# Delta rule: where a tile's convolution and the values' eviction stand in the order of the engines

## The chip, the cores and the metric

The kernel runs on one core of a Trainium2 chip. The core has TensorE (PE, matrix products), VectorE (DVE), ScalarE (ACT), GpSimd (POOL) and SyncE (SP, which issues DMA transfers); each executes its own queue in order, and semaphores tie the queues together. The metric is the device time of one execution, in microseconds (us): 3261.68 as the median of 3 runs (3260.92 to 3266.36).

## The reference, cut to what matters

One inference step of a two-layer recurrent trunk, over a prompt of 2048 tokens and 8 sample tokens. The first layer (gated linear attention beside a state-space model) is not touched. The second layer is a gated delta rule with 8 heads of width 128:

```
qkv, z, b, a = split((h @ w_in).astype(f32), ODD_SIZES)
qkv, conv_new = causal_conv(qkv, s_conv, conv_w)     # depthwise, width 4
qkv = silu(qkv)
q, k, v = split(qkv);  q = l2norm(q) * DN_DK ** -0.5;  k = l2norm(k)
beta = sigmoid(b);  g = -exp(a_log) * softplus(a + dt_bias)
# per chunk of tokens:
lower = where(strict, beta * (k k^T) * decay, 0)
sol = triangular_solve(lower + eye, [v * beta, k * beta * exp(gcum)])
v_new = u_v - w_k S
o = (q * exp(gcum)) S + (q k^T * decay) v_new
S = S * exp(g_last) + (k * exp(g_last - gcum))^T v_new
out = (rmsnorm(o) * silu(z)) @ w_out
```

## The kernel before, in words

The prompt is cut into four blocks of four chunks of 128 tokens. The first block also carries the 8 sample tokens, so its dense products run in two sub-tiles of 264 and 256 columns; the others have one sub-tile of 512. A step is one head of one block: 32 steps, heads 0 to 7 of each block. Weights and activations are split in a high and a low half, so a dense product of 8 blocks of the inner dimension is 24 matrix multiplications per sub-tile (`dense_steps`; `Hh`, `Hl` are the activations, `whl` the weights).

`dn_dense` makes, for one step, four products in the order k, q, v, z. For k, q and v, `project` allocates the tile `pre`, copies the three columns before the block into it (`pre<-halo`, L1675; in the first block also `pre<-cst`, L1673), lets ACT evict the product from PSUM into it (L1682), and then makes the convolution: one scaled copy on ACT (L1690), three multiply-adds on DVE (L1692, tile `yc`), a tanh on ACT (L1695, tile `th`, which shares its two buffers with `pre`), and the product that gives `kT`, `qT` or `vT` (L1696). So a next `pre` can be filled only when the convolution before has read the buffer two allocations back. The products use two PSUM banks (`pmm`): PE can start a sub-tile only when the one two before it has been evicted.

`dn_prefix` (per step) turns kT by PE transposes, builds `MT`, sends a diagonal `md` through DRAM and back (`LB`), and runs a chain of 30 small DVE instructions (`t`, `u`). `dn_inverse` makes the triangular inverse, `dn_queries` turns qT and vT by PE transposes into `ptp` banks (two of them) and evicts the values as `vtok` (L1838), `dn_chain` runs the chunk recurrence (`pch`, `ppo`, `xx`, `dS`), and `dn_sample` treats the sample tokens (its states are updated by eight DVE instructions, `sbuf`, L2037).

The order on PE is fixed by a planner (`Weave`): each piece of work is a generator that yields what it waits for, and the planner runs the next one that is due on a clock that counts PE work alone, at 2400 columns per us; `weave.post(key, after)` makes a piece due `after` us of that clock later, with numbers from the table `LAT`. In `dense_steps` each of the 8 steps of a sub-tile yields once. The order on the other engines comes from the scheduler of the framework, which places an instruction by priority and its own timing; `in_turn()` takes that freedom from an instruction: it may not be placed ahead of the DVE instruction that was given out last before it. `after(steps, late)` runs a product and, once four yields have passed with something in the list `late`, gives out the first entry of that list.

Of the kernel before, what the change touches and what calls it, by code (L numbers as in the profile page):

```python
# [12 lines left out]
F32 = mybir.dt.float32  # L13
# [4 lines left out]
AF = mybir.ActivationFunctionType  # L18
OP = mybir.AluOpType
# [4 lines left out]
P = 128  # L24
D = 1024
KD = 8
EPS = 1e-6
NSM = 8
# [7 lines left out]
C3 = float(np.float32(TWO_PI - C1 - C2))  # L36
MAGIC = 12582912.0

LAT = dict(gates=11, conv=5, kconv=8, snorm=5.25, z=2.04, tp=3, qtp=1, mt=18, grow=5, blocks=9, sub=3, dve=1.02, act=0.675,
           gchain=0.9, gload=1.2, gsample=15, columns=0.9, hout=3, gsplit=3.57, inv1=1.53, inv2=1.3, inv3=0.9,  # L40
           inv4=0.837, inv5=0.796, inv6=0.972, chain1=0.972, chain2=0.729, chain3=0.837, split=1.95, sload=2.66,
           cout=2.25, norm=5.5, load=2, us=3.74, sq=4, out=3.24, entry=9.6, x=1.88, gentry=7.98, make=30, far=8,
# [97 lines left out]
def tile_trunk(ctx, tc, A, O):  # L140
    nc = tc.nc
# [6 lines left out]
    TG = NSM + P * GBLK[0][1]  # L148
# [99 lines left out]
    convw = cvec[:, 19:115].rearrange("p (i t) -> p t i", t=24)  # L248
# [384 lines left out]
    weave = Weave(tc, pe)  # L633
# [916 lines left out]
    w_odd = A["w_in_odd"][0]  # L1550
    dS, keep = [], {}
# [106 lines left out]
    def dn_dense(dp, blk, h, g):  # L1658
        hi, lo = H[blk]
        ns, off, T, subs = bounds(blk)  # L1660
        nch = blk[1]
        X0 = NX if ns else 3
        kT = dp.tile([P, NCG, P], F32, tag="kT", bufs=3, name="kT")
        qT = dp.tile([P, NCG, P], F32, tag="qT", bufs=3, name="qT")
        kqs = dp.tile([P, 3, NSM], F32, tag="kqs", bufs=2, name="kqs") if ns else None
        zs = dp.tile([P, TG], F32, tag="zs", bufs=3, name="zs")
        dd[g] = [kT, qT, kqs, None, zs]

        def project(ti, dst, si):
            pre = dp.tile([P, NX + TG - NSM], F32, tag="pre", bufs=2, name="pre")  # L1670
            W = X0 + nch * P
            if ns:
                nc.vector.tensor_copy(pre[:, :32].rearrange("p (s i) -> p s i", i=4)[:, :, :3],  # L1673
                                      keep["cst"][:, ti].rearrange("p i s -> p s i"))
            nc.vector.tensor_copy(pre[:, X0 - 3:X0], halo[:, :, ti])  # L1675

            def ev(ps, o, w, c, k):
                n0 = ns if c == 0 else 0
                if n0:
# [8 lines left out]
            y = dp.tile([P, NX + TG - NSM], F32, tag="yc", bufs=2, name="yc")  # L1688
            yv = y[:, 3:W]
            nc.scalar.activation(yv, pre[:, 0:W - 3], AF.Copy, scale=convw[:, ti, 0:1])  # L1690
            for i in range(1, 4):
                nc.vector.scalar_tensor_tensor(yv, pre[:, i:W - 3 + i], convw[:, ti, i:i + 1], yv,  # L1692
                                               op0=OP.mult, op1=OP.add)
            t = dp.tile([P, NX + TG - NSM], F32, tag="pre", bufs=2, name="th")
            nc.scalar.activation(t[:, 3:W], yv, AF.Tanh, scale=0.5)  # L1695
            nc.vector.scalar_tensor_tensor(dst, t[:, X0:W].rearrange("p (c t) -> p c t", t=P), 1.0,  # L1696
                                           y[:, X0:W].rearrange("p (c t) -> p c t", t=P),
                                           op0=OP.add, op1=OP.mult)
            if ns:
                s4 = lambda a: a[:, :32].rearrange("p (s i) -> p s i", i=4)[:, :, 3]  # L1700
                nc.vector.scalar_tensor_tensor(kqs[:, si], s4(t), 1.0, s4(y), op0=OP.add, op1=OP.mult)

        yield from project(8 + h, kT[:, :nch], 0)
        weave.post(("k", g), LAT["kconv"])
        yield from project(h, qT[:, :nch], 1)
        weave.post(("q", g), LAT["conv"])
# [3 lines left out]
        yield from project(16 + h, vT[:, :nch], 2)  # L1710
        weave.post(("v", g), LAT["conv"])
# [6 lines left out]
        yield from dense_steps(w_odd[:, 3072 + h * P:3072 + (h + 1) * P], KD, hi, lo, subs, ev_z)  # L1718
        weave.post(("z", g), LAT["z"])

    def tiles_of(n):
# [99 lines left out]
    def dn_queries(dp, blk, h, g):  # L1821

        n = blk[1]
        kT, qT, kqs, vT, zs = dd[g]
        eg, E, ktok, ivr, cb, egl = keys[g]
        T3 = tiles_of(n)
        pt = ptp()
        for c in range(n):
            pe.transpose(pt[:, c * P:(c + 1) * P], qT[:, c], ident)
        rq = norms(pt, n, "sq_")[1]  # L1830
        rq_ = dp.tile([P, NCG], F32, tag="rq", bufs=3, name="rq")[:, :n]
        nc.vector.tensor_scalar(rq_, rq, P ** -0.5, None, op0=OP.mult)
# [5 lines left out]
        nc.vector.tensor_tensor(vtok, pt[:, :n * P].rearrange("p (c t) -> p c t", t=P),  # L1838
                                ivr.unsqueeze(2).to_broadcast([P, n, P]), op=OP.mult)
# [501 lines left out]
```

## Time and profile before

| what | us |
|---|---|
| median of 3 runs | 3261.68 |
| lowest and highest | 3260.92, 3266.36 |
| the profiled execution's own time | 3250.56 |
| its span in the trace | 3248.8 |
| the delta-rule layer's head steps | about 1738 to 3172 |
| of these the first block | about 1738 to 2110 |

The profile is one execution. Its page gives busy times of each engine, its trace every instruction. PE is busy for 91% of the span, DVE for 68%. A wait is shown as the idle time of an engine ahead of an instruction, with the instruction on another engine that ended it. PEclk is the clock that was granted to TensorE: 1.00 is 2.4 GHz, 0.50 is 1.2 GHz.

### The profile page before, as it was taken

The page shows a single profiled execution, that of the slowest core. Times are in us where ns is not written, and L with a number is a line of the kernel's source. Part 1 is how long each engine was busy: PE and PEld are TensorE (multiplying, and loading weights), DVE is VectorE, ACT ScalarE, POOL GpSimd, SP SyncE. Part 2 cuts the span into 40 slices and gives each one's busy share as a digit, 9 for nine tenths or more (in the row PEclk, how much of TensorE's full clock was granted, in tenths as well). Part 3 has the DMA queues.
Part 4 walks back from the last instruction along what each step waited for, and adds up shares of the span by engine and source line. Part 5 has one row for each costly group of instructions (what it writes and reads, how often), then busy time and mean ns, then how long its engine had stood idle before and what let it go on. Part 6 is the DMA issues. An engine that isn't in the chain of part 4 may idle for free.

```text
span 3248.8 us, 53026 instructions
## 1 busy us (share of the span) xinstructions
PE 2955.9 (91%) x18425; PEld 2497.5 (77%) x18425; DVE 2224.4 (68%) x5715; ACT 1255.7 (39%) x3321; POOL 995.0 (31%) x1236
## 2 busy tenths in 40 slices
PE   6888799999999989978988888899998999999998
PEld 5877678777778768877767888877887788787886
DVE  7766556645444546765867888867887678857885
ACT  5443343323323323241134444443444344434442
POOL 6565444322202222240034444431112121211111
PEclk8898899999999999989999999999999999999999
DMA  7565965673483485664466566676444844475446
GB/s 216 190 209 177 297 184 148 190 256 126 136 276 126 133 287 153 200 202 148 155 198 216 172 193 185 190 230 221 139 147 140 270 146 145 125 234 192 141 139 191
DMA packets 398232, 602.96 MB, mean 186 GB/s; under 512 B 62521, under 2 KB 257964, under 8 KB 397828
## 3 DMA queue, kind: packets, MB, share of 16 engines
q1 hardware_dynamic: 394902, 589.98, 57.3%
q0 software_dynamic: 2560, 8.42, 0.9%
q8 instruction: 145, 2.38, 0.3%
q10 hardware_dynamic: 502, 1.17, 0.1%
q14 instruction: 123, 1.01, 0.1%
HBM read 433.31 MB, written 166.34 MB: 185 GB/s over the span
## 4 chain that ended last, share of the span: by engine, by line
PE 35%; DVE 15%; DMA 4%; issue 3%; ACT 2%; POOL 1%; SPq 0%; POOLq 0%; DVEq 0%; ACTq 0%
PE pmm L93 23%; PE prc L93 5%; PE ptp L97 2%; PE pch L93 2%; DVE yc L1692 2%; PE ppo L93 2%; DVE z L1237 1%; DVE z L1247 1%; DVE Hl L649 1%; DMA out<-yt 1%; DMA LB<-md_d 1%; DVE z L1243 1%; DMA whl<-split 1%; DVE z L1238 0%; DVE z L1248 0%
## 5 line engine op out<-in xcount | busy, mean ns | idle before, releaser
L93 PE MATMUL pmm<-Hh,whl 128*128 128x512 f32 (+4 forms) x5200 | 1597.3, 370 | 42.8 <-ACT pre L1682 13.2
L93 PEld LDWEIGHTS pmm<-Hh,whl 128*128 128x128 f32 x5200 | 951.2, 193 | 173.8 <-ACT pre L1682 14.8
L93 PE MATMUL pmm<-Hl,whl 128*128 128x512 f32 (+5 forms) x2640 | 937.0, 355 | 5.6 <-DVE Hl L649 4.2
L93 PEld LDWEIGHTS pmm<-Hl,whl 128*128 128x128 f32 (+1 forms) x2640 | 506.5, 192 | 55.6 <-DVE Hl L649 6.0
L93 PE MATMUL pmm<-Oh,whl 128*128 128x512 f32 (+2 forms) x1120 | 354.3, 379 | 30.5 <-DVE res L1064 13.4
L320 POOL TENSOR_TENSOR whl<-raw,whl 128x512 fp32r<-128x512 f32 (+1 forms) x176 | 232.3, 1322 | 203.9 <-ACT whl L319 194.9
L93 PEld LDWEIGHTS pmm<-Oh,whl 128*128 128x128 f32 x1120 | 211.3, 200 | 65.7 <-DVE res L1064 16.9
L1692 DVE SCALAR_TENSOR_TENSOR yc<-pre,cvec,yc 128x512 f32<-128x512 f32 (+1 forms) x288 | 228.8, 795 | 43.2 <-ACT yc L1690 40.5
L93 PE MATMUL pmm<-Ol,whl 128*128 128x512 f32 (+2 forms) x560 | 203.3, 363 | 0.6 <-DVE Ol L370 0.6
L319 ACT ACTIVATE whl<-raw 128x512 fp32r<-128x512 f32 (+1 forms) x176 | 108.5, 618 | 127.4 <-PE pmm L93 78.0
L93 PEld LDWEIGHTS pmm<-Ol,whl 128*128 128x128 f32 x560 | 112.6, 201 | 11.4 <-DVE Ol L370 1.7
L907 DVE TENSOR_TENSOR dlt<-b 128x512 f32<-128x512 f32 x112 | 87.5, 782 | 39.8 <-ACT E L914 38.9
L93 PE MATMUL pmm<-oh,whl 128*128 128x512 f32 (+3 forms) x320 | 93.6, 370 | 18.3 <-DVE res L1378 15.4
L908 ACT ACTIVATE E<-dlt 128x256 f32<-128x256 f32 x112 | 47.4, 423 | 156.1 <-DVE dlt L907 32.3
L1682 ACT ACTIVATE pre<-pmm 128x512 f32<-128x512 f32 (+1 forms) x120 | 61.1, 510 | 115.4 <-PE pmm L93 115.1
L646 POOL TENSOR_TENSOR xb<-xb,rr 128x1024 f32<-128x1024 f32 (+1 forms) x32 | 76.9, 2412 | 90.9 <-DMA xb<-xs_d 40.4
L1968 ACT ACTIVATE jk<-ppo,rq 128x128 bf16<-128x128 f32 x128 | 46.7, 365 | 140.2 <-PE ppo L93 139.1
L1685 POOL COPY halo<-pre 128x3 f32<-128x3 f32 x96 | 22.3, 232 | 241.0 <-ACT pre L1682 240.3
L1064 DVE TENSOR_TENSOR res<-pmm,res 128x512 f32<-128x512 f32 (+2 forms) x80 | 46.2, 584 | 68.6 <-PE pmm L93 50.0
L1729 ACT ACTIVATE jk<-ptp 128x128 bf16<-128x128 f32 x256 | 70.8, 277 | 53.8 <-PE ptp L97 48.3
L275 POOL TENSOR_TENSOR s<-s,mhalf 128x4 f32<-128x4 f32 (+2 forms) x41 | 40.6, 989 | 162.6 <-DVE s L274 160.7
L1695 ACT ACTIVATE th<-yc 128x512 f32<-128x512 f32 (+1 forms) x96 | 61.0, 635 | 73.1 <-DVE yc L1692 72.8
(1527 smaller groups left out, 6103.8 us busy)
## 6 DMA issues: line engine op xcount, KB each, us to landing
whl<-split SPq DMA_DIRECT2D x460, 512.0 KB
split<-whl SPq DMA_DIRECT2D x168, 512.0 KB
res<-xs_d SPq DMA_DIRECT2D x88, 256.0 KB
sm<-s5m SPq DMA_DIRECT2D x32, 514.0 KB
raw<-in_w_in_even SPq DMA_DIRECT2D x64, 256.0 KB
xs_d<-res SPq DMA_DIRECT2D x64, 256.0 KB
raw<-in_w_in_odd SPq DMA_DIRECT2D x64, 256.0 KB
LB<-md_d SPq DMA_DIRECT2D x64, 256.0 KB
```

The costliest lines, as they stand in the source:

```text
L93: return self.e.matmul(out, w, x, **kw)
L97: return self.e.transpose(out, x, ident)
L319: nc.scalar.activation(t[:, 0, :m], raw, AF.Copy)
L320: nc.gpsimd.tensor_tensor(t[:, 1, :m], raw, t[:, 0, :m].bitcast(F32), op=OP.subtract)
L646: nc.gpsimd.tensor_tensor(xb, xb, rr.unsqueeze(1).to_broadcast(list(xb.shape)), op=OP.mult)
L907: nc.vector.tensor_tensor(d3, b3, b3[:, :, s - 1:s].to_broadcast([P, nb_, 2 * s]), op=OP.subtract)
L908: nc.scalar.activation(E3[:, :, s:], d3[:, :, s:], AF.Exp, scale=IS)
L1682: nc.scalar.activation(pre[:, X0 + c * P:X0 + (c + k) * P], ps[:, n0:], AF.Copy)
L1692: nc.vector.scalar_tensor_tensor(yv, pre[:, i:W - 3 + i], convw[:, ti, i:i + 1], yv, op0=OP.mult, op1=OP.add)
L1695: nc.scalar.activation(t[:, 3:W], yv, AF.Tanh, scale=0.5)
L1729: nc.scalar.activation(jk, pt[:, c * P:(c + 1) * P], AF.Square, accum_out=ss[:, c:c + 1])
L1968: nc.scalar.activation(jk[:rows], po[:rows, c * P:(c + 1) * P], AF.Square, scale=rq[:rows, c:c + 1], accum_out=s1[:, c:c + 1])
```

## The change

Three edits, all in the delta-rule layer.

```diff
-LAT = dict(gates=11, conv=5, kconv=8, ...
+LAT = dict(gates=11, conv=4, kconv=6.5, ...
...
-        def project(ti, dst, si):
-            pre = dp.tile([P, NX + TG - NSM], F32, tag="pre", bufs=2, name="pre")
+        late = []
+
+        def project(ti, dst, si, done):
             W = X0 + nch * P
-            if ns:
-                nc.vector.tensor_copy(pre[:, :32]..., keep["cst"]...)
-            nc.vector.tensor_copy(pre[:, X0 - 3:X0], halo[:, :, ti])
+            pre_ = []
             def ev(ps, o, w, c, k):
+                if c == 0:
+                    pre_.append(dp.tile([P, NX + TG - NSM], F32, tag="pre", bufs=2, name="pre"))
+                pre = pre_[0]
+                if c == 0:
+                    if ns:
+                        nc.vector.tensor_copy(pre[:, :32]..., keep["cst"]...)
+                    nc.vector.tensor_copy(pre[:, X0 - 3:X0], halo[:, :, ti])
...
-            yield from dense_steps(w_odd[:, ti * P:(ti + 1) * P], KD, hi, lo, subs, ev)
+            yield from after(dense_steps(w_odd[:, ti * P:(ti + 1) * P], KD, hi, lo, subs, ev), late)
...
+            def turn():
                 nc.scalar.activation(yv, pre[:, 0:W - 3], AF.Copy, scale=convw[:, ti, 0:1])
-            for i in range(1, 4):
+                with in_turn():
+                    nc.vector.scalar_tensor_tensor(yv, pre[:, 1:W - 2], convw[:, ti, 1:2], yv, ...)
+                for i in range(2, 4):
                     nc.vector.scalar_tensor_tensor(yv, pre[:, i:W - 3 + i], convw[:, ti, i:i + 1], yv, ...)
...
+                weave.post((done, g), LAT["kconv" if done == "k" else "conv"])
+            late.append(turn)
...
-        yield from dense_steps(w_odd[:, 3072 + h * P:...], KD, hi, lo, subs, ev_z)
+        yield from after(dense_steps(w_odd[:, 3072 + h * P:...], KD, hi, lo, subs, ev_z), late)
...
             pe.transpose(pt[:, c * P:(c + 1) * P], vT[:, c], ident)
-        nc.vector.tensor_tensor(vtok, pt[...], ivr..., op=OP.mult)
+        yield LAT["qtp"]
+        with in_turn():
+            nc.vector.tensor_tensor(vtok, pt[...], ivr..., op=OP.mult)
```

The convolution of a product is given out at the fourth yield of the product behind it (k's amid q, q's amid v, v's amid z); its first DVE instruction may not stand ahead of DVE work given out until then. `pre` is allocated, and its halo copied, at the first eviction. The planner's due time for kT is now 6.5 us of its clock after that fourth yield (before: 8 after the product's end), for qT and vT 4 (before: 5). The eviction `vtok` is given out one due time (`qtp`, 1 us) after vT's transposes, and marked in the same way; the product of q and k that follows it moves with it. Every engine executes the same instructions as before; only their order differs. In the changed kernel L1692 is L1702 and L1705, L1675 is L1684, L1838 is L1853, L2037 is L2052.

The order on PE, head 0 of the first block, from the last matrix multiplication of v's product (256 columns) to vT's transposes, before:

```order
L93 MATMUL pmm<-Hh,whl 128x256
L93 MATMUL pmm<-Hh,whl 128x264
L93 MATMUL pmm<-Hl,whl 128x264
L93 MATMUL pmm<-Hh,whl 128x264
L97 MATMUL ptp<-ident,vT 128x128 x4
L93 MATMUL prc<-qT,kT 128x128 x4
```

and now, with z's first sub-tile (264 columns) from its third multiplication on:

```order
L93 MATMUL pmm<-Hh,whl 128x264
L97 MATMUL ptp<-ident,qT 128x128 x4
L93 MATMUL pmm<-Hh,whl 128x264
L93 MATMUL pmm<-Hl,whl 128x264
L93 MATMUL pmm<-Hh,whl 128x264 x2
L93 MATMUL pmm<-Hl,whl 128x264
L93 MATMUL pmm<-Hh,whl 128x264 x2
L93 MATMUL pmm<-Hl,whl 128x264
L93 MATMUL pmm<-Hh,whl 128x264 x2
L93 MATMUL pmm<-Hl,whl 128x264
L93 MATMUL pmm<-Hh,whl 128x264
L97 MATMUL ptp<-ident,vT 128x128 x4
```

Before, vT's transposes stood 3 multiplications behind the end of v's product; now they stand 15 behind it.

The order on DVE, head 1 of the first block, from q's convolution to the halo copy that lets v's product be evicted, before (`sbuf` are the sample states of head 0):

```order
L1692 SCALAR_TENSOR_TENSOR yc<-pre,cvec,yc 128x544
L2037 SCALAR_TENSOR_TENSOR sbuf__17516<-sbuf__17516,egs,sbuf__17517 128x128 x8
L1692 SCALAR_TENSOR_TENSOR yc<-pre,cvec,yc 128x544
L1731 TENSOR_SCALAR sk__17820<-sk__17820 128x4
L1776 TENSOR_TENSOR ktok<-ptp,E 128x512
L1692 SCALAR_TENSOR_TENSOR yc<-pre,cvec,yc 128x544
L1673 COPY pre<-cst 128x8x3
L1675 COPY pre<-halo 128x3
```

and now, the rows from these sample states to q's convolution:

```order
L2052 SCALAR_TENSOR_TENSOR sbuf__17510<-sbuf__17510,egs,sbuf__17511 128x128 x8
L1709 SCALAR_TENSOR_TENSOR kT<-th,yc 128x512
L1828 TENSOR_TENSOR t__17557<-LB,u__17555 128x4x5
L370 TENSOR_TENSOR Ol<-og,Oh 128x8
L1714 SCALAR_TENSOR_TENSOR kqs<-th,yc 128x8
L1768 COPY egs<-gr 128x8
L1771 COPY egl<-gr 128x4
L1702 SCALAR_TENSOR_TENSOR yc<-pre,cvec,yc 128x544
L1830 TENSOR_TENSOR u__17555<-u__17555,t__17557 128x4x5
L2029 TENSOR_TENSOR kq<-i_75,kqs 128x2x32
L1705 SCALAR_TENSOR_TENSOR yc<-pre,cvec,yc 128x544
```

The eight updates of the sample states stood between the first and the second multiply-add of q's convolution; now they stand ahead of kT, and of q's convolution.

The order on DVE, head 1 of the first block, from vT to vtok before:

```order
L1696 SCALAR_TENSOR_TENSOR vT<-th,yc 128x512
L1701 SCALAR_TENSOR_TENSOR kqs<-th,yc 128x8
L1799 TENSOR_TENSOR lb<-MT,blkd 128x512
L1716 SCALAR_TENSOR_TENSOR zs<-thr,pmm 128x264
L1801 TENSOR_REDUCE md<-lb 128x64
L1731 TENSOR_SCALAR sq__17959<-sq__17959 128x4
L1716 SCALAR_TENSOR_TENSOR zs<-thr,pmm 128x256
L1838 TENSOR_TENSOR vtok<-ptp,ivr 128x512
L1832 TENSOR_SCALAR rq<-rn 128x4
L1845 TENSOR_TENSOR kq__17999<-prc,E 128x512
```

and now, the rows that end in vtok and U:

```order
L1993 TENSOR_TENSOR on<-so,s_18169 8x128
L1830 TENSOR_TENSOR u__18061<-u__18061,t__18063 128x4x4
L1948 SCALAR_TENSOR_TENSOR xx__18221<-pch,neg,vtok 128x128
L1828 TENSOR_TENSOR t__18063<-LB,u__18061 128x4x3
L1830 TENSOR_TENSOR u__18061<-u__18061,t__18063 128x4x3
L1828 TENSOR_TENSOR t__18063<-LB,u__18061 128x4x2
L1830 TENSOR_TENSOR u__18061<-u__18061,t__18063 128x4x2
L1828 TENSOR_TENSOR t__18063<-LB,u__18061 128x4
L1830 TENSOR_TENSOR u__18061<-u__18061,t__18063 128x4
L1853 TENSOR_TENSOR vtok<-ptp,ivr 128x512
L1873 TENSOR_TENSOR U<-blkd,u__18061 128x512
```

The eviction of the values stood seven rows behind vT, ahead of the chain of `t` and `u`; now it stands behind that chain.

## Rows read from the trace of the kernel before

**Rows 1.** Busy time by stretch: columns in the heading line.
```profile
core 0: us, PE busy (x) PEld busy (x) DVE busy (x) ACT busy (x) POOL busy (x), PEclk, DMA share, GB/s
1738.00:2110.00 372.00, 323.22 (x2755) 305.05 (x2755) 320.97 (x935) 171.72 (x541) 170.83 (x183) 0.96 0.60 188
2430.00:2610.00 180.00, 165.63 (x973) 133.75 (x971) 122.88 (x309) 72.66 (x196) 32.33 (x38) 0.98 0.63 201
2610.00:2790.00 180.00, 179.50 (x1217) 150.75 (x1216) 145.99 (x424) 79.92 (x243) 34.17 (x45) 1.00 0.47 143
```

**Rows 2.** Waits of PE, 1735 to 2110: us in total, times, longest.
```profile
PE pmm L93 <- ACT pre L1682: 13.2, 5, 6.7
PE pch L93 <- DVE dS L1950: 8.5, 7, 2.4
...
PE ptp L97 <- DVE vT L1696: 2.7, 1, 2.7
```

**Rows 3.** Waits of PE, 2610 to 2790.
```profile
PE ppo L93 <- ACT jk L1968: 0.3, 1, 0.3
```

**Rows 4.** Waits of DVE, 1735 to 2110.
```profile
DVE yc L1692 <- ACT yc L1690: 9.7, 7, 6.2
DVE vtok L1838 <- PE ptp L97: 3.9, 3, 1.7
```

**Rows 5.** Timeline of DVE, start of the first block: start, us, instruction, idle before.
```profile
1734.27 1.28 DVE L1692 SCALAR_TENSOR_TENSOR yc<-pre,cvec,yc 128x544 f32<-128x544 f32 x1 [6.21 <-ACT yc L1690]
```

**Rows 6.** Timeline of PE, head 0 of the first block.
```profile
1754.30 0.28 PE L93 MATMUL pmm<-Hh,whl 128*128 128x264 f32 x1
1757.31 1.11 PE L97 MATMUL ptp<-ident,vT 128*128 128x128 f32 x4 [2.73 <-DVE vT L1696]
```

**Rows 7.** Timeline of PE, head 1 of the first block.
```profile
1777.04 0.28 PE L93 MATMUL pmm<-Hl,whl 128*128 128x264 f32 x1
...
1777.40 0.28 PE L93 MATMUL pmm<-Hl,whl 128*128 128x264 f32 x1
...
1782.64 0.28 PE L93 MATMUL pmm<-Hh,whl 128*128 128x256 f32 x1
1789.58 0.59 PE L93 MATMUL pmm<-Hh,whl 128*128 128x264 f32 x1 [6.66 <-ACT pre L1682]
```

**Rows 8.** Timeline of DVE, heads 0 and 1 of the first block.
```profile
1757.26 0.41 DVE L1716 SCALAR_TENSOR_TENSOR zs<-thr,pmm 128x256 f32<-128x256 f32 x1
...
1776.78 0.16 DVE L1675 COPY pre<-halo 128x3 f32<-128x3 f32 x1
...
1781.50 1.82 DVE L1692 SCALAR_TENSOR_TENSOR yc<-pre,cvec,yc 128x544 f32<-128x544 f32 x1
1783.24 3.19 DVE L2037 SCALAR_TENSOR_TENSOR sbuf__17516<-sbuf__17516,egs,sbuf__17517 128x128 f32<-128x128 f32 x8
...
1788.68 0.16 DVE L1675 COPY pre<-halo 128x3 f32<-128x3 f32 x1
```

**Rows 9.** Busy time by stretch, around two PE waits: columns as in Rows 1.
```profile
1749.80:1756.60 6.80, 4.27 (x34) 3.85 (x33) 6.76 (x15) 2.65 (x9) 1.78 (x2) 1.00 0.70 228
1756.60:1763.40 6.80, 6.09 (x28) 5.84 (x29) 4.30 (x10) 1.08 (x5) 4.25 (x4) 0.50 0.61 161
1787.30:1794.10 6.80, 4.53 (x21) 4.53 (x22) 5.85 (x16) 2.54 (x7) 3.06 (x4) 0.50 0.75 226
```

**Rows 10.** Timeline of DVE and PE, first head of the second block.
```profile
2188.97 0.67 DVE L1696 SCALAR_TENSOR_TENSOR vT<-th,yc 128x512 f32<-128x512 f32 x1
...
2199.30 0.60 PE L97 MATMUL ptp<-ident,vT 128*128 128x128 f32 x4
```

**Rows 11.** The line of vtok: who waited for it; the list is empty.
```profile
who waited for it (us, times):
busy tenths in 40 slices 0000000000000000000000000000000000000000
```

**Rows 12.** The line of t: one head's 15 instructions, first and last start.
```profile
L1815 DVE TENSOR_TENSOR t__18084<-LB,u__18082 x15: 163/180/222, 1803.8 to 1815.0; 128x60 f32<-128x60 f32 x1, 128x56 f32<-128x56 f32 x1, 128x52 f32<-128x52 f32 x1, 128x48 f32<-128x48 f32 x1
```

More of the change, by code (lines that the diff above doesn't have):

```diff
@@ L37 @@
 MAGIC = 12582912.0
-LAT = dict(gates=11, conv=5, kconv=8, snorm=5.25, z=2.04, tp=3, qtp=1, mt=18, grow=5, blocks=9, sub=3, dve=1.02, act=0.675,
+LAT = dict(gates=11, conv=4, kconv=6.5, snorm=5.25, z=2.04, tp=3, qtp=1, mt=18, grow=5, blocks=9, sub=3, dve=1.02, act=0.675,
            gchain=0.9, gload=1.2, gsample=15, columns=0.9, hout=3, gsplit=3.57, inv1=1.53, inv2=1.3, inv3=0.9,
@@ L1682, in ev @@
                 nc.scalar.activation(pre[:, X0 + c * P:X0 + (c + k) * P], ps[:, n0:], AF.Copy)
-            yield from dense_steps(w_odd[:, ti * P:(ti + 1) * P], KD, hi, lo, subs, ev)
+            yield from after(dense_steps(w_odd[:, ti * P:(ti + 1) * P], KD, hi, lo, subs, ev), late)
+            pre = pre_[0]
             nc.gpsimd.tensor_copy(halo[:, :, ti], pre[:, W - 3:W])
@@ L1687, in project @@
                 nc.gpsimd.tensor_copy(keep["cnew"][:, ti], pre[:, :32].rearrange("p (s i) -> p s i", i=4)[:, :, 3])
-            y = dp.tile([P, NX + TG - NSM], F32, tag="yc", bufs=2, name="yc")
-            yv = y[:, 3:W]
-            nc.scalar.activation(yv, pre[:, 0:W - 3], AF.Copy, scale=convw[:, ti, 0:1])
-            for i in range(1, 4):
-                nc.vector.scalar_tensor_tensor(yv, pre[:, i:W - 3 + i], convw[:, ti, i:i + 1], yv,
-                                               op0=OP.mult, op1=OP.add)
@@ L1694, in project @@
[L1694 to L1706, printed above, removed]
+            def turn():
+                y = dp.tile([P, NX + TG - NSM], F32, tag="yc", bufs=2, name="yc")
+                yv = y[:, 3:W]
+                nc.scalar.activation(yv, pre[:, 0:W - 3], AF.Copy, scale=convw[:, ti, 0:1])
+                with in_turn():
+                    nc.vector.scalar_tensor_tensor(yv, pre[:, 1:W - 2], convw[:, ti, 1:2], yv,
+                                                   op0=OP.mult, op1=OP.add)
+                for i in range(2, 4):
+                    nc.vector.scalar_tensor_tensor(yv, pre[:, i:W - 3 + i], convw[:, ti, i:i + 1], yv,
+                                                   op0=OP.mult, op1=OP.add)
+                t = dp.tile([P, NX + TG - NSM], F32, tag="pre", bufs=2, name="th")
+                nc.scalar.activation(t[:, 3:W], yv, AF.Tanh, scale=0.5)
+                nc.vector.scalar_tensor_tensor(dst, t[:, X0:W].rearrange("p (c t) -> p c t", t=P), 1.0,
+                                               y[:, X0:W].rearrange("p (c t) -> p c t", t=P),
+                                               op0=OP.add, op1=OP.mult)
+                if ns:
+                    s4 = lambda a: a[:, :32].rearrange("p (s i) -> p s i", i=4)[:, :, 3]
+                    nc.vector.scalar_tensor_tensor(kqs[:, si], s4(t), 1.0, s4(y), op0=OP.add, op1=OP.mult)
+                weave.post((done, g), LAT["kconv" if done == "k" else "conv"])
@@ L1707, in dn_dense @@
+            late.append(turn)
+        yield from project(8 + h, kT[:, :nch], 0, "k")
+        yield from project(h, qT[:, :nch], 1, "q")
         if g:
@@ L1709, in dn_dense @@
         dd[g][3] = vT = dp.tile([P, NCG, P], F32, tag="vT", bufs=1, name="vT")
-        yield from project(16 + h, vT[:, :nch], 2)
-        weave.post(("v", g), LAT["conv"])
+        yield from project(16 + h, vT[:, :nch], 2, "v")
         def ev_z(ps, o, w, c, k):
@@ L1716, in ev_z @@
             nc.vector.scalar_tensor_tensor(zs[:, o:o + w], thr, 1.0, ps, op0=OP.add, op1=OP.mult)
-        yield from dense_steps(w_odd[:, 3072 + h * P:3072 + (h + 1) * P], KD, hi, lo, subs, ev_z)
+        yield from after(dense_steps(w_odd[:, 3072 + h * P:3072 + (h + 1) * P], KD, hi, lo, subs, ev_z), late)
         weave.post(("z", g), LAT["z"])
@@ L1837, in dn_queries @@
             pe.transpose(pt[:, c * P:(c + 1) * P], vT[:, c], ident)
-        nc.vector.tensor_tensor(vtok, pt[:, :n * P].rearrange("p (c t) -> p c t", t=P),
-                                ivr.unsqueeze(2).to_broadcast([P, n, P]), op=OP.mult)
+        yield LAT["qtp"]
+        with in_turn():
+            nc.vector.tensor_tensor(vtok, pt[:, :n * P].rearrange("p (c t) -> p c t", t=P),
+                                    ivr.unsqueeze(2).to_broadcast([P, n, P]), op=OP.mult)
         weave.post(("vT", g))
```

4 lines of the change are left out of this document (2 added, 2 removed).

## The prediction

> **What bounds the kernel now.** I read the busy times by stretch first, then the waits of PE, then those of DVE, and the timelines of the longest waits last. The change touches only the head steps of the delta-rule layer, from 1738 us on, and these fall into three kinds. In the inner heads of the later blocks PE is busy for 179.50 of 180 us [rows 1], and its longest wait there adds up to 0.3 us [rows 3]: PE's own instructions are the limit, and none of them is removed. In the first block PE is busy for 323.22 of 372 us and DVE for 320.97 [rows 1], so PE stands still for 48.8 us; DVE carries the sample tokens there, and the two engines wait for each other in turn. At a change of block PE loses 14.4 of 180 us [rows 1]. So the 48.8 us of the first block are what an order can win or lose, with less at three changes of block.
>
> Of these 48.8, the list of waits names 13.2 us in five waits for the eviction into `pre`, 8.5 for the state update and 2.7 for vT [rows 2]. DVE itself waits there 9.7 us for ACT's scaled copy at the head of a convolution and 3.9 us for vT's transposes ahead of vtok [rows 4]. The longest of the former, 6.21 us, is at the block's start, where nothing else is ready [rows 5].
>
> **The change part by part.** Nothing is removed and nothing added, no transfer either: the convolution issues none, and the weight loads on SP are issued when a product's generator starts, as before. POOL's halo copy stays at the product's end. What remains is who waits for whom.
>
> *vT against its transposes.* At head 0 PE waits 2.73 us for vT [rows 6]. The transposes move from 3 to 15 multiplications behind v's product. Three of 264 columns take 1777.40 - 1777.04 = 0.36 us [rows 7], so 12 take 1.44 us. On DVE an eviction of 0.41 us (zs, 256 columns [rows 8]) now stands ahead of vT. The wait becomes 2.73 - 1.44 + 0.41 = 1.7 us: a gain of 1.0. In later heads, PE's row moves back by a similar amount and DVE's by less, except at first heads of a block: there vT goes behind last rows of the output of the block before. In the second block the slack is 2199.30 - (2188.97 + 0.67) = 9.7 us [rows 10], and I count nothing.
>
> *The banks of the products.* At head 1 PE waits 6.66 us for a bank [rows 7]: z's first sub-tile needs the one that v's first left, its eviction needs the halo copy, and that needs q's three multiply-adds. On DVE 11.9 us pass from one halo copy to the next (1776.78 to 1788.68), 3.19 of them in the eight sample-state updates [rows 8]. In the new order these eight stand between the same two halo copies, only earlier, ahead of kT. So the content between the copies is the same, give or take one instruction of half a microsecond, and I take 0 for all five waits. Bounds: all 13.2 us go [rows 2], or the updates delay each of the seven other heads as they do here, 7 x 3.19 = 22 us.
>
> *kT.* Its transposes are due 2.56 + 6.5 = 9.06 us of the planner's clock behind the product (12 multiplications of 512 columns at 2400 columns per us, then the new number) instead of 8. At head 1 the updates now stand ahead of it, 3.19 us [rows 8], where the spare time is of that order. I charge +1.0, between -1.1 (the later due time) and +3.2.
>
> *DVE's own idle time.* A first multiply-add that stands behind work given out until the fourth yield finds ACT's copy finished more often, and a vtok that stands later finds its transposes. In the first block that can return 9.7 - 6.2 = 3.5 and 3.9 us [rows 4, 5], 7.4 together. PE is busy for 87% there and DVE for 86%, so I let half reach the end: -3.7, between 0 and -7.4. Where PE is full, the same idle time is worth nothing.
>
> *vtok.* At head 1 it now stands behind the whole chain of `t` and `u`, whose first and last `t` start 11.2 us apart [rows 12]. Until then one of the two transpose banks stays full. Behind vT's transposes come those of the sample's k, q and v and then those of `on`; the latter must wait for vtok. But the DVE row that writes this `on` stands only nine rows ahead, and at the other seven heads vtok stands ahead of it. Price: between 0 and 2.3 us (0.67 for an instruction of 512 columns [rows 10] and eight short rows between at about 0.2 each, as the `t` are [rows 12]); I take 0, since before nobody waited for vtok [rows 11]. The Trainium skill ("PSUM — Partial Sum Buffer", "Summary: rules for kernel authors") says to evacuate promptly, because the memory is tight, and so speaks against this edit. The trace, with an empty list of waiters, does not yet show the case in which it bites; by that rule head 1 would pay the 2.3.
>
> *Changes of block and the tail.* No row that I have puts the 14.4 us down to a convolution; behind the last product the order on PE differs by single groups of three multiplications. I take 0, between -4 (a quarter of one 14.4) and +4.
>
> Sum: -1.0 + 0 + 1.0 - 3.7 + 0 + 0 = -3.7 us. The profiled execution takes 3250.56 us (span 3248.8 and 1.8 around it) and would become 3246.9. It is 11.1 us under the median of the runs, to which the same difference applies: 3261.68 - 3.7 = 3258.0.
>
> **The rivals.**
>
> *Faster: the long waits go, and the slow clock with them.* After the wait at head 0 the granted clock is 0.50 for 6.80 us, after that of head 1 again for 6.80, where the stretch before stood at 1.00 with PE busy for only 4.27 of 6.80 [rows 9]. At 1.2 instead of 2.4 GHz half of the busy time there is lost: (6.09 + 4.53) / 2 = 5.3 us. If the new order frees the banks in time, 13.2 + 2.7 + 5.3 = 21 us are won, 3240; with half of it 3251. For it: DVE's order is what the waits name. Against it: the rows between two halo copies hardly change. The Trainium skill ("TensorE: Matmul & The Clock Gate", "What's actually happening") calls the throttled clock the default, which activity releases; by that each long wait that goes pays twice, and this is the case in which it does. The trace agrees in these two stretches.
>
> *Slower: the convolution stands too far back.* This is one mechanism: the mark puts the first multiply-add behind the `t`, `u` chain, the sample-state updates or a wait for LB that were given out before it; the next halo copy, and with it the eviction, comes later, and PE finds no bank. It decides when DVE's rows between two halo copies exceed PE's two sub-tiles. One update set costs 3.19 us [rows 8], and the slow clock behind it (6.80 us, 4.53 of them busy [rows 9]) 2.3 more. On three of the first block's heads that is 3 x 5.5 = 16 us, 3278; on two, 3273. For it: DVE has little idle time there. Against it: the scheduler had placed these rows similarly.
>
> *It moves, but nothing sees it.* In the 24 later heads that is already the forecast; if it holds in the first block too, the time is 3262.
>
> **How the numbers follow.** About 0.2%, 6.5 us, is what a measurement of this kernel can tell from no change. The forecast with the fourth case (3253 to 3267) has 0.42. The faster rival, in full or half, has 0.36, the slower one 0.22. The signs follow: faster 0.36, same 0.42, slower 0.22. The range of 8 in 10 takes in the full gain less a little and the two-head loss: 3241 to 3275; the likeliest case's own is 3253 to 3267.
>
> **What the changed profile would show.** Right: waits of PE for vT at head 0 of about 1.7 us; waits for `pre` in the first block near 13 us; idle time of DVE ahead of its first multiply-add and of vtok down by some 7 us; PE still full in the inner heads. Wrong: `pre` waits under 5 us or over 20 us; PE waiting ahead of `on` at head 1 for vtok; PE idle in the inner heads, where I expect none.

## The result, and the profile after

The changed kernel takes 3275.01 us as the median of 9 runs (3265.28 to 3277.56), the kernel before 3258.79 in 9 runs beside it: a ratio of 1.0051, 95% interval 1.0034 to 1.0068. It is slower by 0.5%, some 16 us; I had forecast 3.7 us less. The profiled execution of the changed kernel (3265.28 us, mean granted clock 0.966) is the fastest of its nine; the other eight have 0.960 to 0.962.

The start of each block's gates (`bcol`, L1644) cuts the head steps into the four blocks. The timeline of DVE, before (start, us, instruction, idle before):

```profile
1735.55 0.31 DVE L1644 COPY bcol<-ptp 128x160 f32<-128x160 f32 x1
2155.12 0.32 DVE L1644 COPY bcol<-ptp 128x160 f32<-128x160 f32 x1 [0.68 <-PE ptp L97]
2503.93 0.33 DVE L1644 COPY bcol<-ptp 128x160 f32<-128x160 f32 x1 [1.96 <-PE ptp L97]
2858.59 0.31 DVE L1644 COPY bcol<-ptp 128x160 f32<-128x160 f32 x1
```

and after:

```profile
1729.26 0.55 DVE L1644 COPY bcol<-ptp 128x160 f32<-128x160 f32 x1
2162.50 0.33 DVE L1644 COPY bcol<-ptp 128x160 f32<-128x160 f32 x1
2514.79 0.31 DVE L1644 COPY bcol<-ptp 128x160 f32<-128x160 f32 x1
2872.76 0.31 DVE L1644 COPY bcol<-ptp 128x160 f32<-128x160 f32 x1
```

The first block is 433.2 us long instead of 419.6, the second 352.3 instead of 348.8, the third 358.0 instead of 354.7, and the rest to the end of the span (3263.6 and 3248.8) 390.8 instead of 390.2. That is some 21 us more in the head steps; the stretch ahead of them, which the change does not touch, was some 6 us shorter in this execution.

Waits of PE after, 1738 to 2110 (us in total, times, longest), which answer to [rows 2]:

```profile
PE pmm L93 <- ACT pre L1688: 23.6, 7, 6.6
PE ppo L93 <- ACT jk L1983: 10.1, 6, 3.0
PE pch L93 <- DVE dS L1965: 7.2, 4, 3.1
PE ptp L97 <- DVE kT L1709: 3.8, 1, 3.8
PE ptp L97 <- DVE vT L1709: 3.7, 2, 2.0
```

The waits for a bank have grown from 13.2 to 23.6 us. The longest, in head 4, on PE and on DVE:

```profile
1916.10 0.28 PE L93 MATMUL pmm<-Hh,whl 128*128 128x256 f32 x1
1923.01 0.59 PE L93 MATMUL pmm<-Hh,whl 128*128 128x264 f32 x1 [6.64 <-ACT pre L1688]
```

```profile
1913.47 4.22 DVE L2052 SCALAR_TENSOR_TENSOR sbuf__19423<-sbuf__19423,egs,sbuf__19424 128x128 f32<-128x128 f32 x6 [1.79 <-POOL sbuf__19424 L2050]
1917.89 0.60 DVE L2052 SCALAR_TENSOR_TENSOR sbuf__19423<-sbuf__19423,egs,sbuf__19424 128x128 f32<-128x128 f32 x2
1918.42 0.77 DVE L1702 SCALAR_TENSOR_TENSOR yc<-pre,cvec,yc 128x544 f32<-128x544 f32 x1
...
1920.40 1.60 DVE L1705 SCALAR_TENSOR_TENSOR yc<-pre,cvec,yc 128x544 f32<-128x544 f32 x2
...
1922.60 0.16 DVE L1684 COPY pre<-halo 128x3 f32<-128x3 f32 x1
```

DVE waits 1.79 us for POOL, updates the sample states, and only then begins k's convolution (1918.42); the halo copy for q's `pre` follows at 1922.60, and PE goes on at 1923.01. This looks like my slower rival. The experiments show that the mark, which puts the convolution there, is not what made the block longer.

In the later blocks PE waits for vT. Waits of PE after, 2125 to 3180:

```profile
PE ptp L97 <- DVE vT L1709: 15.0, 9, 4.2
...
PE ptp L97 <- DVE kT L1709: 2.5, 2, 1.8
```

Before, neither stands in the list of that stretch. DVE's waits, 1735 to 2110: vtok is no longer in the list, and ahead of the first multiply-add of a convolution, where [rows 4] has 9.7 us, there stands:

```profile
DVE yc L1702 <- ACT yc L1700: 2.3, 4, 1.1
```

The stretches that answer to [rows 1]:

```profile
1738.00:2110.00 372.00, 311.71 (x2660) 294.22 (x2658) 317.55 (x915) 163.03 (x521) 162.09 (x175) 0.95 0.57 179
2430.00:2610.00 180.00, 169.78 (x1024) 138.27 (x1023) 128.46 (x321) 74.98 (x203) 33.80 (x39) 0.99 0.65 207
2610.00:2790.00 180.00, 179.44 (x1241) 150.58 (x1239) 144.67 (x421) 81.10 (x248) 32.77 (x45) 1.00 0.46 144
```

The stretch 2610 to 2790 is as full as before. I had taken it for all inner heads; the second block's are not like it.

### The profile page after: what moved, and what is told of

Read it like the earlier page. It is cut to its first block, busy times and chain, and to the rows that moved or that the text cites. A ratio compares the mean times of both kernels' runs of the same rounds, so it can differ in the third digit from the quotient of the medians.

```text
span 3263.6 us, 53061 instructions
## 1 busy us (share of the span) xinstructions
PE 2947.5 (90%) x18425; PEld 2489.9 (76%) x18425; DVE 2228.7 (68%) x5715; ACT 1250.1 (38%) x3321; POOL 992.5 (30%) x1236
## 4 chain that ended last, share of the span: by engine, by line
PE 35%; DVE 15%; DMA 4%; issue 3%; ACT 3%; POOL 2%; SPq 0%; POOLq 0%; DVEq 0%; ACTq 0%
PE pmm L93 24%; PE prc L93 5%; PE ptp L97 2%; PE pch L93 2%; PE ppo L93 2%; DVE Hl L649 1%; DVE yc L1705 1%; DVE z L1237 1%; DVE z L1247 1%; DMA LB<-md_d 1%; ACT jk L1742 1%; DVE z L1243 1%; DMA xs_d<-res 1%; DVE z L1238 0%; DVE z L1248 0%
## 5 line engine op out<-in xcount | busy, mean ns | idle before, releaser
L93 PE MATMUL pmm<-Hh,whl 128*128 128x512 f32 (+4 forms) x5200 | 1600.1, 370 | 53.4 <-ACT pre L1688 23.6
L1705 DVE SCALAR_TENSOR_TENSOR yc<-pre,cvec,yc 128x512 f32<-128x512 f32 (+1 forms) x192 | 149.2, 777 | 3.3
L93 PE MATMUL pmm<-oh,whl 128*128 128x512 f32 (+3 forms) x320 | 91.9, 365 | 15.6 <-DVE res L1378 13.2
L1692 POOL COPY halo<-pre 128x3 f32<-128x3 f32 x96 | 27.8, 289 | 244.7 <-ACT pre L1688 237.2
L1953 ACT ACTIVATE ww<-pch,cb 128x128 f32<-128x128 f32 x128 | 46.7, 365 | 137.8 <-PE pch L93 135.3
L1742 ACT ACTIVATE jk<-ptp 128x128 bf16<-128x128 f32 x256 | 70.5, 275 | 64.0 <-PE ptp L97 58.5
```

Of the source, the lines that this page charges most:

```text
L93: return self.e.matmul(out, w, x, **kw)
L1742: nc.scalar.activation(jk, pt[:, c * P:(c + 1) * P], AF.Square, accum_out=ss[:, c:c + 1])
L1953: nc.scalar.activation(ww, ch[:, P:2 * P], AF.Copy, scale=cb[:, c:c + 1])
```

## The experiments

Eighteen kernels ran. The block lengths are of each one's profiled execution, taken as above. The median less the sum of the four lies between 1734 and 1746 us for all twenty kernels, so a sum is good to some 5 us against the medians, and a block not better. `a_` kernels start from the changed kernel, `b_` kernels from the one before; the text gives the base of the others.

| kernel | 1st | 2nd | 3rd | 4th to end | median | ratio to before, 95% |
|---|---|---|---|---|---|---|
| before | 419.6 | 348.8 | 354.7 | 390.2 | 3254 to 3259 | 1 |
| after | 433.2 | 352.3 | 358.0 | 390.8 | 3275.0 | 1.0034 to 1.0068 |
| a_nomark | 435.5 | 343.5 | 354.3 | 390.1 | 3261.1 | 1.0002 to 1.0026 |
| a_markns | 432.2 | 351.7 | 356.9 | 390.2 | 3272.5 | 1.0035 to 1.0070 |
| a_lat | 435.3 | 350.1 | 355.1 | 390.9 | 3266.8 | 1.0018 to 1.0048 |
| a_vtokold | 426.6 | 366.7 | 364.9 | 399.6 | 3294.2 | 1.0103 to 1.0135 |
| a_inpl | 444.3 | 355.4 | 360.2 | 392.9 | 3289.9 | 1.0094 to 1.0135 |
| b_inpl | 429.3 | 348.5 | 354.3 | 390.2 | 3257.6 | 0.9984 to 1.0025 |
| b_vtoknew | 442.0 | 347.3 | 355.4 | 390.5 | 3277.3 | 1.0053 to 1.0086 |
| b_vtokyield | 441.6 | 344.4 | 354.8 | 390.8 | 3271.8 | 1.0032 to 1.0070 |
| b_vtokmark | 429.8 | 347.2 | 353.3 | 390.6 | 3261.0 | 1.0000 to 1.0028 |
| o_gate | 431.1 | 347.6 | 355.3 | 392.2 | 3270.9 | 1.0033 to 1.0066 |
| o_delay | 430.1 | 346.7 | 353.8 | 391.3 | 3256.3 | 0.9988 to 1.0018 |
| o_kqlate | 440.8 | 347.5 | 356.0 | 393.2 | 3273.0 | 1.0034 to 1.0077 |
| o_vtoklate | 428.5 | 346.7 | 350.9 | 389.2 | 3260.2 | 1.0002 to 1.0035 |
| m_later | 436.1 | 340.4 | 352.5 | 388.4 | 3260.8 | 1.0005 to 1.0033 |
| o_late | 430.2 | 346.6 | 355.3 | 392.5 | 3261.3 | 0.9998 to 1.0033 |
| m_best | 422.5 | 340.2 | 353.5 | 389.6 | 3249.2 | 0.9966 to 0.9992 |
| m_best2 | 424.4 | 343.3 | 351.6 | 396.1 | 3258.9 | 0.9995 to 1.0025 |
| m_mark | 422.0 | 348.0 | 359.4 | 390.9 | 3260.6 | 1.0000 to 1.0028 |

**The mark on the convolution.** a_nomark takes it off everywhere, a_markns in the first block only:

```diff
-                with in_turn():                                  # after
+                with (in_turn() if not ns else ExitStack()):     # a_markns
```

> The changed kernel with the mark taken off the convolution's first multiply-add (its late giving out, the due times and the vtok edit stay). Theory A, the mark: in heads 2 to 7 of the first block it puts the convolution behind the eight sample-state updates, so the halo copy and the eviction come later and PE finds no bank. Then the waits of PE for `pre` in the first block fall from 23.6 us to about 13 (as before the change), and the time from 3275 to about 3259 +- 4. Theory B, the late giving out: half a product of delay is what makes the convolution late, mark or not. Then the waits stay at 20 us or more and the time at 3271 to 3278.

> The changed kernel with the mark on the convolution only in the blocks without samples (second to fourth). Theory A: the loss sits in the first block, so this is worth as much as taking the mark off everywhere: 3259 +- 4, `pre` waits of the first block about 13 us. Theory C, the later blocks lose too by the mark (their waits for vT, 4.8 + 4.8 us between 2300 and 2640, come from the marked start of v's convolution): then the kernel without any mark is faster than this one by 5 us or more. Theory B: 3271 to 3278.

Without the mark the kernel is 14 us faster than after, as theory A had it, but not where: the first block stays at 435.5 us, and the second and third give back 8.8 and 3.7. Its waits for `pre`, 1738 to 2110, stay as well:

```profile
PE pmm L93 <- ACT pre L1688: 22.1, 7, 5.6
```

PE's waits for vT after 2125 us are gone. With the mark kept in the later blocks alone nothing is won (3272.5), and these waits are 13.8 us again. Theory A falls, and so does my slower rival as the cause: the mark costs in the later blocks, where PE waits for vT. m_mark repeats this on the best kernel (below).

**The due times.** a_lat has `conv=5, kconv=8` again.

> The changed kernel with the due times of before (conv 5 and kconv 8 instead of 4 and 6.5), counted from the later giving out. Theory D: the waits of PE for kT, qT and vT from the second block on (some 17 us in the trace of the changed kernel, under 2 before it) come from due times that are too short by about a microsecond; then they fall under 5 us, the first block keeps its 23.6 us for `pre`, and the time falls by 5 to 12 us, to 3263 to 3270. Rival: PE, with nothing else to run there, waits for another thing instead: 3275 +- 3.

The waits for vT after 2125 us fall from 15.0 to 3.4, the time by 8 us, inside what was forecast. But the second and third block win only 2.2 and 2.9, and in the waits jk (8.2 us) and ww (4.9) stand in vT's place: half theory D, half its rival.

**The banks of the products.** The tanh is written over `pre`, so that two products in a row use different buffers:

```diff
-                t = dp.tile([P, NX + TG - NSM], F32, tag="pre", bufs=2, name="th")
+                t = pre
```

> The changed kernel with the tanh written over `pre` instead of into a next buffer of it, so that the next product's `pre` takes the other buffer and its eviction no longer waits for the convolution before. Theory H, the shared buffers: it is by them that a later convolution keeps PE from a bank; the first block's waits for `pre` fall from 23.6 us to under 8, the first block (first `bcol` to second `bcol`) from 433 us to under 420, the time to 3255 or less. Rival I: DVE is simply late in the first block, and the eviction finds another wait (halo copy behind other DVE rows): the block stays at 428 or more, the time at 3270 to 3278.

> The kernel before with the tanh written over `pre`. Theory H: its 13.2 us of waits for `pre` in the first block fall under 5, and the slow clock behind them goes too: the first block from 420 us to 400 to 410, the time to 3240 to 3250. Rival I: 3255 to 3259, as before.

The waits for `pre` are gone, but the first block of a_inpl is 444.3 us long. Its waits of PE, 1738 to 2110, from the longest on:

```profile
PE ptp L97 <- DVE on L1993: 15.5, 4, 5.9
PE ppo L93 <- ACT jk L1983: 10.1, 6, 3.0
PE pch L93 <- DVE dS L1965: 6.7, 4, 3.2
PE ptp L97 <- DVE kT L1709: 6.7, 3, 4.7
```

Now PE waits for `on`, the normalised output. In b_inpl the waits for `pre` are gone too, `on` (11.5 us) leads the list instead, and the kernel is as fast as before: in the first block PE stands still for 52.6 us instead of 54.5. (The profiled block is longer, 429.3 us, at a granted clock of 0.92 instead of 0.95, but over all executions the mean clock is that of before, 0.9639 in 12 and 0.9637 in 23.) So the wait for a bank was where PE happened to stand, not what it lacked. Theory H falls, and with it the faster rival of the prediction, which counted on freed banks for 21 us.

**The values' eviction.** a_vtokold undoes the vtok edit in the changed kernel, b_vtoknew makes it alone in the kernel before.

> The changed kernel with the eviction vtok given out as before, right behind vT's transposes and without a mark. Theory E: the late vtok holds a transpose bank and the chain's xx behind the t, u chain; then waits of PE for xx and for ACT's jk fall (10.1 us for jk in the first block, 6.4 before the change) and the time falls by 4 to 8 us, to about 3269. Theory A or B: vtok plays no part, 3275 +- 3.

> The kernel before with the vtok edit alone (given out one due time later, marked). The run without this edit was slower by some 20 us than the changed kernel, so the edit gives back time beside the late convolution. Theory F: it helps by itself, since DVE no longer stops at vtok for vT's transposes: 3250 or less, against 3255 to 3259 before. Rival G: it only repairs what the late convolution breaks (vT comes late, and an unmarked vtok waits for it in front of DVE's other work); by itself it is within 0.2% of before.

Neither came as expected, and together they show that the edits are not additive. Alone the vtok edit makes the first block 22 us longer and leaves the others; beside the late, marked convolution it costs 433.2 - 426.6 = 6.6 us in the first block and saves 14.4 + 6.9 + 8.8 = 30 us behind it. Two halves of it, each in the kernel before:

```diff
+        yield LAT["qtp"]                # b_vtokyield; b_vtokmark has only the mark on the next instruction
         nc.vector.tensor_tensor(vtok, ...)
```

> The kernel before with half of the vtok edit: the eviction vtok, and the product of q and k behind it, are given out one due time later, without the mark. The whole edit alone made the first block (first `bcol` to second `bcol`) 442 us long instead of 420, and the time 3277. Theory J, the giving out: with the yield other generators give out DVE work and PE work ahead of vtok and of the q-k product; then the block is 435 us or more here too, the time 3270 or more. Theory K, the mark: it is the mark that puts vtok, and by it xx and the chunk recurrence, behind the t, u chain; then this kernel is as before, 418 to 424 us and 3255 to 3260.

> The kernel before with the other half: vtok marked, given out where it was, right behind vT's transposes. Theory K, the mark: first block 435 us or more, time 3270 or more. Theory J, the giving out: 418 to 424 us, 3255 to 3260. If both halves are needed (the mark holds vtok behind what the yield let others give out), neither run is over 428.

The yield alone gives 441.6 us and 3272: theory J. The mark alone may cost 10 us of block and shows 5 in the time, at the edge of what can be told. Behind the yield stand vtok with the key `vT`, which releases the next v product, the product of q and k (`kq`), the scaling of q on POOL, and the key `queries`, which releases the next head's prefix and the recurrence. o_gate keeps the yield but releases the prefix early, o_delay delays the key alone; o_kqlate puts the yield between vtok and the product, o_vtoklate puts vtok behind the product and the yield. All four start from the kernel before. The scaling of q and the key `queries` are late in both of the last two, so what differs there is the product against vtok and its key:

```diff
         nc.vector.tensor_tensor(vtok, ...)
         weave.post(("vT", g))
+        yield LAT["qtp"]                # o_kqlate
...
-        weave.post(("queries", g), LAT["dve"])
+        weave.post(("queries", g), LAT["dve"] + LAT["qtp"])     # o_delay
```

> The kernel before with the yield ahead of vtok (first block 442 us instead of 420), and the next head's decay and prefix released by a key of their own, posted ahead of that yield, as early as before. Theory N, the planner's gate: the yield posts `queries` later, for which the next head's prefix waits; so kT's transposes and the t, u chain of each next head start later. Then the first block returns to 418 to 426 us and the time to 3255 to 3260. Rival O: the product of q and k, or the eviction itself, comes too late for the chunk recurrence; the block stays at 435 or more, time 3268 to 3275.

> The kernel before, in which only the key `queries` (that releases the chunk recurrence of this head and the prefix of the next) is posted 1 us of the planner's clock later; vtok and the product of q and k stay where they were. Theory N: the first block is 435 us or more, time 3268 or more. Rival O: 418 to 424 us, 3255 to 3260.

> The kernel before, with vtok where it was and the product of q and k (and its eviction, and the key `queries`) one due time later. With vtok late as well the time was 3272 and the first block 442 us; with the key alone late it was 3256, so the gate is not the cause. Theory Q, the product of q and k: it stands later among other work of PE, and the recurrence and the output behind it with it; time 3266 or more, first block 435 us or more. Rival V, vtok: 3255 to 3261, 418 to 430 us.

> The kernel before, with the product of q and k at once behind vT's transposes, and the eviction vtok one due time behind it (the key that releases the next v product comes with it). Rival V: time 3266 or more, first block 435 us or more. Theory Q: 3255 to 3261, 418 to 430 us.

By their times the gate falls twice (3270.9 with it early, 3256.3 with it late); both profiled first blocks, 431 and 430, lie between the theories. The later product costs nearly all of it: 440.8 us and 3273.0, against 428.5 and 3260.2 for the later vtok. The waits of PE in o_kqlate, 1738 to 2150:

```profile
PE ptp L97 <- DVE on L1979: 13.3, 5, 4.3
PE pch L93 <- DVE dS L1951: 7.7, 6, 2.2
PE prc L93 <- DVE Tm L1877: 6.6, 4, 2.1
PE pmm L93 <- ACT pre L1682: 5.0, 2, 4.5
```

Where [rows 2] is led by `pre`, now `on` leads. The waits for `pre` are shorter than before the change, and the block is 21 us longer. Nobody waits for `kq` itself: in all eight heads of the block its eviction ends 43 us or more ahead of the `ppo` multiplication that reads it first. What has grown most is not a wait. The first block as one stretch (columns as in [rows 1]), before, in o_kqlate and in the changed kernel:

```profile
1735.55:2155.12 419.57, 365.08 (x3066) 342.99 (x3064) 351.53 (x998) 195.00 (x596) 191.53 (x198) 0.95 0.61 192
1739.34:2180.19 440.85, 380.51 (x3067) 355.85 (x3065) 354.87 (x999) 191.92 (x596) 189.31 (x198) 0.91 0.58 183
1729.26:2162.50 433.24, 362.70 (x3046) 339.19 (x3045) 358.86 (x996) 194.74 (x594) 192.80 (x200) 0.95 0.58 183
```

Of the 21.3 us of o_kqlate, 15.4 are PE busy for longer with the same multiplications, at a mean granted clock of 0.91 instead of 0.95, and only 5.9 are idle time. One profile alone would not show it, since b_inpl's block had a clock of 0.92 too, but here the other executions agree: o_kqlate has 0.9588 on average in 6, the kernel before 0.9642 in 17 beside them. PE is busy for 2956 us before; at the lower clock that work would take some 17 us longer (an estimate from these numbers), and the medians differ by 18.6. b_vtokyield has 0.9597, but o_vtoklate 0.9627 and o_delay 0.9637. So most of what the later product costs is a lower granted clock of PE; why its place in PE's order lowers the clock is not shown. In the changed kernel's profile the loss of the block looks different: the clock is 0.95 as before, and PE's idle time has grown from 54.5 to 70.5 us.

**Late convolution and best version.** These five start from the changed kernel. m_later gives the convolution out late, unmarked, in the later blocks only; m_best also keeps the vtok edit to these, m_best2 leaves it out everywhere, o_late has the convolution late in all blocks and the vtok edit in the later ones, and m_mark is m_best with the mark:

```diff
+            if ns:                      # m_later, m_best, m_best2, m_mark: first block
+                turn()
+            else:
                 late.append(turn)
...
+        if not blk[0] == 0:             # m_best, m_mark, o_late: later blocks
             yield LAT["qtp"]
+        with (in_turn() if not blk[0] == 0 else ExitStack()):
             nc.vector.tensor_tensor(vtok, ...)
```

> The changed kernel without the mark on the convolution, and with the late giving out (and the shorter due times) in the second to fourth blocks only; in the first block the convolution is given out at the product's end with due times 8 and 5, `pre` still at the first eviction. Theory B (as the runs have left it: the first block loses by the late giving out, the later blocks by the mark): the first block returns from 435 us to 420, the later blocks stay at 343, 354 and 390, so the time is 3250 +- 4, below before. Rival: the first block loses by `pre` at the first eviction or by the marked vtok: it stays at 430 or more, the time at 3261.

> The convolution given out late without a mark, and the vtok edit, both in the second to fourth blocks only (the first block keeps due times 8 and 5; `pre` is allocated at the first eviction everywhere). Theory L: the first block's loss is the vtok edit's, so it returns from 436 us to 418 to 424, and the later blocks keep the 340, 352 and 388 us that the late unmarked convolution gave: time 3240 to 3250, faster than before. Rival M: the first block loses by `pre` at the first eviction: it stays at 430 or more, time 3258 to 3262.

> As the run beside it, but without the vtok edit in any block: only the late, unmarked convolution in the later blocks. If the vtok edit matters only beside a marked convolution, this equals the other, 3240 to 3250, with later blocks of 340, 352, 388 us. If vtok given out at once stops DVE for a vT that now comes later (as without the edit in the changed kernel: 367, 365 and 400 us), the later blocks are 10 us or more longer in sum than with the edit, and the time 3255 or more.

> The convolution given out late, unmarked, in all blocks; the vtok edit in the second to fourth only. Against the run with both in the later blocks only (first block 422.5 us, time 3249) this shows what the late convolution costs in the first block by itself. Theory P: it costs there what the changed kernel keeps when the vtok edit is undone, 427 - 420 = 7 us: first block 427 to 432, time 3253 to 3258. Rival: without the vtok edit the late convolution costs nothing, 420 to 424 us, time 3247 to 3251.

> The fastest kernel so far (late convolution without a mark, and the vtok edit, both in the second to fourth blocks only: 340, 353 and 390 us) with the mark put on the convolution in these blocks. Theory C, the mark makes PE wait for vT there: the blocks become 350, 357 and 390 us as in the changed kernel, waits of PE for vT from under 2 to 13 us or more, the time 3259 to 3266. Rival: the mark costs only together with a late first block: 3249 +- 3.

m_later won in the later blocks (12 us of block lengths against before) and nothing in the first, since the vtok edit was still there; m_best returns the first block to 422.5 us and beats both kernels: 3249.21 us, ratio 0.9979 (0.9966 to 0.9992). It is the only one of the eighteen whose interval lies under 1. Between the two only the vtok edit in the first block differs, and again most of the difference is PE's busy time and clock there (m_best, then m_later):

```profile
1742.19:2164.74 422.55, 366.84 (x3069) 343.31 (x3068) 349.92 (x1000) 195.40 (x597) 192.03 (x198) 0.96 0.62 192
1744.13:2180.27 436.14, 376.92 (x3067) 353.10 (x3066) 351.94 (x999) 192.50 (x595) 192.09 (x198) 0.92 0.58 184
```

Without the vtok edit (m_best2) 10 us of m_best are lost, 6.5 of them in the last block of its one profile: there the edit seems to pay. What the late convolution costs in the first block by itself stays open: o_late has 430.2 - 422.5 = 8 us more there and 12 us more time than m_best, above theory P's 3253 to 3258, but 11 of the 19 us by which its blocks are longer lie in the later ones, where both kernels have the same edits; and beside the vtok edit it costs nothing (a_nomark 3261.1, m_later 3260.8). And the mark alone costs 7.8 us in the second block, 5.9 in the third, 11 in the time. How it does so, at the third block's first head, on DVE and PE, with the mark:

```profile
2562.73 0.75 DVE L1702 SCALAR_TENSOR_TENSOR yc<-pre,cvec,yc 128x512 f32<-128x512 f32 x1
...
2564.43 0.75 DVE L1705 SCALAR_TENSOR_TENSOR yc<-pre,cvec,yc 128x512 f32<-128x512 f32 x1
...
2567.79 0.22 DVE L1831 TENSOR_TENSOR t__27055<-LB,u__27053 128x60 f32<-128x60 f32 x1 [2.61 <-DMA LB<-md_d]
2567.92 0.75 DVE L1705 SCALAR_TENSOR_TENSOR yc<-pre,cvec,yc 128x512 f32<-128x512 f32 x1
...
2569.47 0.69 DVE L1709 SCALAR_TENSOR_TENSOR vT<-th,yc 128x512 f32<-128x512 f32 x1
```

```profile
2570.21 1.11 PE L97 MATMUL ptp<-ident,vT 128*128 128x128 f32 x4 [3.25 <-DVE vT L1709]
```

and without it (m_best):

```profile
2555.28 0.68 DVE L1708 SCALAR_TENSOR_TENSOR vT<-th,yc 128x512 f32<-128x512 f32 x1
...
2565.54 0.22 DVE L1830 TENSOR_TENSOR t__27055<-LB,u__27053 128x60 f32<-128x60 f32 x1 [3.60 <-DMA LB<-md_d]
```

```profile
2563.91 0.60 PE L97 MATMUL ptp<-ident,vT 128*128 128x128 f32 x4
```

The mark starts v's convolution so late that its third multiply-add falls behind `t`, the instruction in which DVE waits for the transfer of LB. Unmarked, vT is finished 9.6 us before that `t` starts, and PE finds it ready. PE's waits for vT in m_mark, 2125 to 3180 (in m_best there are none):

```profile
PE ptp L97 <- DVE vT L1709: 13.7, 9, 3.2
```

Only two of the nine, at the first heads of the third and fourth block (3.25 and 3.14 us), stand behind a wait for LB. The five of the second block, 6.5 us together, do not. What the later blocks share is the delay itself: over their 24 heads, the first multiply-add of v's convolution starts on average 4.5 us after ACT's scaled copy with the mark and 0.5 without, and vT is finished 1.1 us ahead of its transposes instead of 4.9.

## Why the prediction was wrong

- **The step that failed first: vtok.** I took 0, at most 2.3 us, for its lateness and for a transpose bank. That price was not paid: nobody waits for vtok in the changed kernel either, and PE does not wait for the `on` that stands ahead of head 1's vtok. I had written that the product of q and k moves with it, and charged nothing. That product is what costs: alone 3273.0 - 3254.4 = 18.6 us in the kernel before (o_kqlate), most of it by a lower granted clock. In the changed kernel the product was not separated from the rest of the edit. Step by step, from the best kernel to the changed one, the ratios to before are 0.9979 (m_best), 1.0019 with the vtok edit in the first block too (m_later), 1.0014 with the late convolution there too (a_nomark), 1.0051 with the mark (after). So the vtok edit in the first block is worth some 13 us of loss and the mark some 12.
- **The second: later heads.** "PE's row moves back by a similar amount and DVE's by less" was said of the heads of the first block and, unchecked, of 24 others; from one slack of 9.7 us [rows 10] and one full stretch [rows 3] I counted nothing. The mark takes that slack: 15.0 us of waits for vT in the changed kernel; by itself 13.7 us of waits and 11 us in time (m_mark).
- **The banks.** Taken as 0, the waits grew to 23.6 us, over the 20 that I named as wrong, and the longest, in head 4, looks like the mechanism of the slower rival. Yet without them nothing is won (a_inpl), and without the mark they stay at 22.1. The rival had the sign, not the cause; its time, two or three heads, 3273 to 3278, agrees with 3275 by accident.
- **DVE's own idle time.** The wait at the block's start [rows 5] now stands ahead of another instruction (5.4 us ahead of `rsd`); of the other 3.5 us ahead of a first multiply-add 2.3 are left, and the 3.9 ahead of vtok are gone: 5.1 us, where I expected some 7. None of it can be found in the block, where DVE's idle time as a whole rose from 68.0 to 74.4 us: other waits took the place of these. The -3.7 should have been 0.
- **vT at head 0** waits 2.01 us (expected 1.7, before 2.73): right. **kT** waits 3.77 us at head 1, above my +3.2. The 9.06 us for its due time was also misread: it holds for sub-tiles of 512 columns, but the first block's have 264, so 12 multiplications are 1.32 us and the sum is 7.82, earlier than the 8 before and not later.
- **What I missed on the good side.** The late, unmarked convolution and the vtok edit together save 10.4 us in the later blocks (m_best), the convolution alone 2.7 (m_best2). In the changed kernel the mark takes this back and more.

Open: why PE is granted less clock when the product of q and k stands later, and how the late convolution, the vtok edit and the planner's order together make the changed kernel's first block longer; the longest waits name places, not the path from one head to the next. Nor is it shown why the second block waits for vT in its inner heads and the third hardly does.

## What to carry over

When two engines wait for each other, the longest wait names the place where one stands, not what it lacks: take the wait away before you explain a loss by it, and compare the engine's busy time and granted clock as well as its waits. Count every instruction that a yield moves, not only the one that it was meant for. A mark that forbids an instruction to move forward must be checked against the time that its consumer has to spare, in every kind of block, and most of all where a wait for a DMA stands ahead in the same queue: here the same edits, unmarked, won in the three later blocks and lost in the first.

## What was not expected of the hardware

That an order of the same instructions can cost by the granted clock more than by waits: 0.9588 on average in o_kqlate, 0.9642 in the kernel before beside it. The spread of the measurement goes the same way: executions of one kernel differ by 20 us (before: 3244 to 3268 in 30 runs; the shortest has a mean granted clock of 0.966, the longest 0.962), and the untouched stretch ahead of the head steps alone by 13 (first `bcol` at 1729.26 in the changed kernel, 1742.2 in m_best), so a difference of 10 us between two single profiles must be looked for in its block and confirmed in medians.
